# The second half of the sample's mLSTM states: from TensorE in the mixers to VectorE in the MLP

## The chip, the cores and the metric

The kernel runs on one core of a Trainium2 chip. The metric is the device time of one execution in microseconds (us); lower is better. The engines are called by their names in the profile: PE is TensorE (matmuls; PEld its weight loads), DVE is VectorE, ACT is ScalarE, POOL is GpSimd, SP is SyncE, which issues nearly all DMAs here.

## The reference, cut to what matters

One layer of a hybrid decoder runs on 256 prompt tokens and on 8 samples of 8 new tokens each, 320 columns in all. Two mixers (mLSTM with 4 heads, HGRN2 with 8) read one input projection; their gated outputs are merged and projected, and an MLP with a layer norm before and after follows:

```python
proj = jnp.einsum('btd,de->bte', x, w_in)
...
h, C, n, m = _mlstm(q, k, v, ig, lf, C0.astype(f32), n0.astype(f32), m0.astype(f32))
...
x1 = _layernorm(DEEPNORM_ALPHA * x + mix, ln1_g, ln1_b)
hid = jnp.square(jax.nn.relu(jnp.einsum('btd,df->btf', x1, w_up)))
ff = jnp.einsum('btf,fd->btd', hid, w_down)
y = _layernorm(DEEPNORM_ALPHA * x1 + ff, ln2_g, ln2_b)
return y, C.astype(dt), n.astype(dt), m.astype(dt), S.astype(dt)
```

The change is about the state C of the mLSTM. Each sample and each head has one of 256 x 512 (key x value). It is read for the outputs, and its new value is an output of the layer:

```python
num = jnp.einsum('bhts,bhsv->bhtv', s, vc) + w_inter[..., None] * jnp.einsum('bhtk,bhkv->bhtv', qc, C)
...
C_new = decay[..., None, None] * C + jnp.einsum('bhs,bhsk,bhsv->bhkv', w_end, kc, vc)
```

For a sample the sum over s has 8 terms, its 8 new tokens. Nothing else in this execution uses C_new.

## The kernel before, in words

All large products are made of tiles: 128 output channels by 320 columns, contracted over 2048 in 16 steps k. fp32 accuracy comes from splitting each operand into a high and a low part, so a step is three matmuls (high x high, low x high, high x low), called main matmuls below. There are 304 tiles (`TILES`): the mixers' projections and gates first, then the branch and output projections, then the MLP in four rounds of 16 up tiles and 16 down tiles. A tile's weights come in two units of 128 x 1024. A unit is loaded into one of three raw buffers (`wr`), ScalarE makes its high part and VectorE subtracts for its low part (`prep` and `low_half`). The pairs of high and low go into three buffers (`wh`, `wl`); from the output projection on, five more pairs (`wx`, tile `bb`) are used as well. `give` hands a pair back after its last matmul.

Everything else is written as Python generators (chains) and put between the main matmuls by `Sched`, a planner that runs when the program is built. It keeps an expected time for each engine, takes the chains in order of priority, and lets an instruction through when the engine and the operands are expected to be free. What it makes is a fixed order for each engine; the chip then goes by semaphores.

For each mLSTM head, the sample's part goes as follows. `m_states` loads the head's states in 16 chunks of 128 x 512 (8 samples times the first or second 128 rows, c = 0 or 1) into a pool of 14 buffers `cb`; from the second head on, two loads are 2.6 us apart. `m_KW` and `fourfold` bring the weighted keys of the samples to tokens in rows, four times over, in `kst`. `m_sample` then issues two lumps, each for four samples: some small sums (`m_few`), eight products of queries with the chunks (the matmuls `bank<-f` and `bank<-rx,f` of 512 columns), and `m_sums`, four matmuls of 32 rows that give the outer products of keys and values for c = 0 in four banks. `m_update` lets VectorE put each into its chunk (decay times chunk plus sum), then issues `m_sums` again for c = 1 into the same banks, and updates those chunks. `m_store` writes each chunk out.

At the end of the program `m_C` makes the prompt's final C from all 256 keys and values, which it loads through GpSimd's queue: heads 0 and 1 into freed weight buffers of `bb` and `wh`, `wl`, heads 2 and 3 into `wr` after the last weights are split.

Of the kernel before, what the change touches and what calls it, by code (L numbers as in the profile page):

```python
# [151 lines left out]
class Sched:  # L152
    PE_SIDE = 900.0

# [17 lines left out]
    def step(self, c, now):  # L172
        if c.req is None:
            try:
                c.req = c.gen.send(c.send)
            except StopIteration:
                c.done = True
                return False
            c.send = None
        kind = c.req[0]  # L180
        if kind == "wait":
            for e in c.req[1]:
                if e.t is None:
                    return False
            c.ready = max([c.ready] + [e.t for e in c.req[1]])
            c.eng = None
        elif kind == "acq":
            pool, n = c.req[1], c.req[2]
            if len(pool.free) < n:
                return False  # L190
            pool.free.sort(key=lambda x: x[0])
            got, pool.free = pool.free[:n], pool.free[n:]
            c.ready = max([c.ready] + [x[0] for x in got])
            c.eng = None
            c.send = got[0][1] if n == 1 else [x[1] for x in got]
        elif kind == "rel":
            c.req[1].free.append((c.ready, c.req[2]))
        elif kind == "set":
            c.req[1].t = c.ready
        else:  # L200
            _, cost, fn, *after = c.req
            r = max(after[0]) if after else c.ready
            if c.eng != kind or after:
                r += LAT
            elif kind in ("act", "dve"):
                r += SAME
            if kind == "pe":
# [9 lines left out]
            end = self.use(kind, r, cost)  # L217
            fn()
            c.ready, c.eng, c.send = end, kind, end
        c.req = None  # L220
        return True
# [20 lines left out]
def wait(*evs):  # L242
    return ("wait", evs)
# [60 lines left out]
class Program:  # L304
# [49 lines left out]
    def carve(self):  # L354
# [39 lines left out]
        self.kst = Pool([R.three(2, 256)])  # L394
# [82 lines left out]
    def carve_b(self):  # L477

        self.bb = self.pool.tile([128, 10240], F32R, name="bb", tag="f1")
        R = self.Part(self.bb)  # L480
        self.bbh, self.bbl = R.three(KT, TOK), R.three(KT, TOK)
        R = self.Part(self.bb)
        wide = [R(2048) for _ in range(5)]
        self.wx = [(w[:, 0:1024], w[:, 1024:2048]) for w in wide]
        self.wxv = wide
# [115 lines left out]
    def give(self, u):  # L601

        now, hl = self.s.t["pe"], self.unit[u][0]
        if FIRST <= u < 2 * FIRST:
            return
        wide = any(hl is w for w in self.wx)
        rest = self.next_prep >= len(UNITS)
        if u + 16 < len(UNITS) or not (rest or (self.n_vx < 3 if wide else self.n_kx < 1)):
            self.hl_free.append((now, hl))
        elif wide:  # L610
            self.n_vx += 1
            self.vx.free.append((now, self.wxv[[hl is w for w in self.wx].index(True)]))
        else:
            self.n_kx += 1
            self.kx.free += [(now, x.rearrange("p (x s k) -> p x s k", x=2, s=2)) for x in hl]
# [16 lines left out]
    def before(self, i, t):  # L632
# [16 lines left out]
        elif kind == "hg" and h == 0:  # L649
# [3 lines left out]
            f2 = self.pool.tile([128, 2320], F32, name="f2l", tag="f2a")  # L653
# [7 lines left out]
        elif kind == "wo" and h == 0:  # L661
# [4 lines left out]
            s.spawn(self.ln_x(), 1)  # L666
        elif kind == "dn" and c == 3 and h == 0:
# [420 lines left out]
    def m_KW(self, h):  # L1088
# [31 lines left out]
        yield from self.fourfold(self.kD[h][256:320], kst)  # L1120
        t = yield acq(self.khl)
        yield from self.high_low(kst.rearrange("p g k -> p (g k)"), t, 0)
# [71 lines left out]
    def m_C(self, h):  # L1194

        late = h >= 2
        if late:

            yield wait(self.rest_ev)
            x = self.wr.rearrange("p u n -> p (u n)")[:, 1536 * (h - 2):1536 * (h - 1)]  # L1200
            xk, xv = x[:, 0:512].rearrange("p (s k) -> p s k", s=2), x[:, 512:1536]
        else:
            k = yield acq(self.kx)
            w = yield acq(self.vx)
            xk, xv = k[:, 1].bitcast(F32), w[:, 1024:2048].bitcast(F32)
        tk = yield ("pool", 1000, lambda: self.nc.gpsimd.dma_start(xk, self.kD[h][0:256].rearrange("(s p) k -> p s k", p=128)))
# [3 lines left out]
        ek, e = Ev(), Ev()  # L1210
        ek.t, e.t = (tk, t + 500.0) if late else (t + 5000.0, t + 5000.0)
        yield wait(ek)
# [3 lines left out]
        if late:  # L1216
            w = yield acq(self.vx)
        yield wait(e)
        yield from self.split(xv, w[:, 0:1024], w[:, 1024:2048], 1024)
# [183 lines left out]
    def m_states(self, h):  # L1403
# [3 lines left out]
        for n in range(2 * NB):  # L1407
            b, c = self.state(n)
            cb = yield acq(self.cb)
            t = yield ("sp", 620, lambda: self.dma(cb, self.d["C0"][h, b, :, 512 * c:512 * c + 512]))  # L1410
# [12 lines left out]
    def m_sums(self, h, n, ps):  # L1423
# [3 lines left out]
        b, c = self.state(n)  # L1427
        g = b // 4
        for x in range(4):
            self.mm(ps[x], kst[32 * x:32 * x + 32, g, 128 * c:128 * c + 128], vst[32 * x:32 * x + 32, g, :], start=True, stop=True)  # L1430

    def m_update(self, h, n, cbs, ps):

        v, m = self.nc.vector, self.mh[h]
        for i in (n, n + 4):
            b, c = self.state(i)
            if i > n:
                yield ("pe", PE_4 + pe_r(512), lambda: self.m_sums(h, i, ps))
            for x in range(4):
                cb, p, bx = cbs[i - n + x], ps[x], b + x  # L1440
                t = yield ("dve", dve(512, True, 1, 1), lambda: v.scalar_tensor_tensor(cb, cb, m["bc"][:, 704 + bx:705 + bx], p, ALU.mult, ALU.add))
                self.s.spawn(self.m_store(h, i + x, cb), 3, t)
        for p in ps:
            yield rel(self.sbank, p)

    def m_store(self, h, n, cb):
        m = self.mh[h]
        b, c = self.state(n)
        yield ("sp", 620, lambda: self.dma(self.d["Cs"][h, b, :, 512 * c:512 * c + 512], cb))
        yield post(m["inter"][n])  # L1450
        yield wait(self.later(2500))
        yield rel(self.cb, cb)

# [842 lines left out]
    def run(self, pool):  # L2296
# [7 lines left out]
        self.wx, self.n_vx, self.n_kx = [], 0, 0  # L2304
# [4 lines left out]
        self.skD = [self.dr.tile([256, 128], F32, name=f"skD{j}") for j in range(HH)]  # L2309
        self.kD = [self.dr.tile([TOK, 256], F32, name=f"kD{j}") for j in range(MH)]  # L2310
# [14 lines left out]
    C0=(MH, NB, 128, 1024), S0=(HH, 128, NB, HV), cst=(128, C_END), lmask=(128, N_MASK),  # L2325
# [3 lines left out]
    Cs=(MH, NB, 128, 1024), Ss=(HH, 128, NB, HV),  # L2329
# [9 lines left out]
def lay_out(x_prompt, x_sample, state_mlstm_C, state_mlstm_n, state_mlstm_m, state_hgrn_S, hg_lb_logits, w_in,  # L2339
# [7 lines left out]
    for n, (i, half) in enumerate(UNITS):  # L2347
# [15 lines left out]
        C0=f(state_mlstm_C)[0].reshape(NB, MH, 2, 128, DV).transpose(1, 0, 3, 2, 4).reshape(MH, NB, 128, 1024),  # L2363
# [3 lines left out]
def take_out(r):  # L2367
# [9 lines left out]
        c(r["Cs"].reshape(MH, NB, 128, 2, DV).transpose(1, 0, 3, 2, 4).reshape(1, NB, MH, DK, DV)),  # L2377
# [21 lines left out]
```

## Time and profile before

| | before |
|---|---|
| median of 3 runs | 2251.0 us (2249.63 to 2251.93) |
| span of the profiled execution | 2246.3 us |
| PE busy | 2240.6 us |
| DVE busy | 1445.7 us |
| ACT busy | 1012.3 us |
| moved by DMA | 432.56 MB, mean 193 GB/s |

The span reaches from the first to the last instruction of one profiled execution; the runs' times hold what lies around it too, and the page gives no other time of that execution. The mixers last until about 810 us, the branch and output projections until about 1320 us, the MLP until 2222 us, and a tail with the final states and the last layer norm until the end. A busy time is the time in which at least one instruction of the engine or group was at work; matmuls overlap, so the distance between two starts tells more of their cost than their duration.

### The profile page before, as it was taken

Reading aid. Unit: us, or ns where it says so; the run is one execution under the profiler, and the core shown is the slowest. Engines: PE = TensorE matmul, PEld = TensorE weight load, DVE = VectorE, ACT = ScalarE, POOL = GpSimd, SP = SyncE. Lnnn points to the kernel's source line nnn. Section 1 sums busy time; section 2 is a strip of 40 time slices with the busy share of each in tenths; the row PEclk is TensorE's granted clock in tenths of the full one; section 3 lists DMA queues with packets and bytes.
Section 4 is the critical chain, followed back from the end, with each engine's and each line's share of the span. In section 5 each row is a group of like instructions: output and inputs, shape, how many; then the busy total and the mean of one; then the engine's idle time right before and its main releaser. Section 6 shows DMA issues by size and latency. Waiting matters only on the chain.

```text
span 2246.3 us, 40624 instructions
## 1 busy us (share of the span) xinstructions
PE 2240.6 (100%) x16218; PEld 2210.0 (98%) x16218; DVE 1445.7 (64%) x2584; ACT 1012.3 (45%) x1527; POOL 21.0 (1%) x53
## 2 busy tenths in 40 slices
PE   9999999999999999999999999999999999999999
PEld 9999999999999999999999999999999999999998
DVE  6768667888888887666556778444444444444566
ACT  5444444554555555444334456333432343234434
POOL 0000000000000000000000000000000000000001
PEclk9999999999999999999999999999999999999999
DMA  7998897776677754444446544444444444444554
GB/s 252 298 279 276 246 289 246 221 238 213 212 232 229 223 188 175 173 173 174 174 174 220 183 144 158 152 148 150 152 150 148 149 151 150 149 149 151 186 170 160
DMA packets 284982, 432.56 MB, mean 193 GB/s; under 512 B 136420, under 2 KB 181744, under 8 KB 284792
## 3 DMA queue, kind: packets, MB, share of 16 engines
q1 hardware_dynamic: 283832, 426.82, 57.3%
q0 software_dynamic: 960, 3.15, 0.5%
q8 instruction: 127, 2.08, 0.3%
q14 instruction: 63, 0.52, 0.1%
HBM read 380.52 MB, written 49.34 MB: 191 GB/s over the span
## 4 chain that ended last, share of the span: by engine, by line
PE 98%; DMA 1%; ACT 0%; SPq 0%; issue 0%; DVE 0%; POOL 0%; ACTq 0%; DVEq 0%; POOLq 0%
PE bank L348 98%; DMA wr<-wt 1%; DMA ra<-kD 0%; SPq L351 0%; ACT wh L342 0%; ACT f L342 0%; DVE wl L520 0%; DVE f L2066 0%; DVE f3m L2241 0%; DVE f2l L2065 0%; ACT misc L342 0%; DVE oS L1832 0%; ACT oS L342 0%; DVE f L966 0%; DVE f L1487 0%
## 5 line engine op out<-in xcount | busy, mean ns | idle before, releaser
L348 PE MATMUL bank<-xh,wh 128*128 128x320 f32 x2408 | 743.7, 310 | 0.0
L348 PE MATMUL bank<-xh,wl 128*128 128x320 f32 x2408 | 743.4, 310 | 0.0
L348 PE MATMUL bank<-xl,wh 128*128 128x320 f32 x2408 | 740.1, 308 | 0.0
L342 ACT ACTIVATE wh<-wr 128x1024 fp32r<-128x1024 f32 x424 | 448.5, 1058 | 588.3 <-PE bank L348 554.9
L520 DVE TENSOR_TENSOR wl<-wr,wh 128x1024 fp32r<-128x1024 f32 x423 | 516.8, 1222 | 293.2 <-ACT wh L342 288.6
L348 PEld LDWEIGHTS bank<-xh,wh 128*128 128x128 f32 x2408 | 452.6, 188 | 5.0 <-issue 3.9
L348 PEld LDWEIGHTS bank<-xl,wh 128*128 128x128 f32 x2408 | 452.1, 188 | 1.9
L348 PEld LDWEIGHTS bank<-xh,wl 128*128 128x128 f32 x2408 | 453.2, 188 | 0.0
L342 ACT ACTIVATE bb<-wr 128x1024 fp32r<-128x1024 f32 x181 | 191.8, 1061 | 353.9 <-PE bank L348 337.7
L520 DVE TENSOR_TENSOR bb<-wr,bb 128x1024 fp32r<-128x1024 f32 x179 | 219.0, 1224 | 157.4 <-ACT bb L342 157.3
L348 PE MATMUL bank<-rxb,bb 128*128 128x320 f32 x1264 | 287.7, 308 | 0.0
L348 PE MATMUL bank<-xh,bb 128*128 128x320 f32 (+1 forms) x1280 | 284.1, 309 | 0.0
L348 PE MATMUL bank<-ra,bb 128*128 128x320 f32 x1112 | 270.5, 308 | 0.0
L348 PE MATMUL bank<-ra,wh 128*128 128x320 f32 x968 | 259.4, 308 | 0.0
L348 PEld LDWEIGHTS bank<-xh,bb 128*128 128x128 f32 x1280 | 214.6, 188 | 0.0
L348 PEld LDWEIGHTS bank<-rxb,bb 128*128 128x128 f32 x1264 | 213.6, 188 | 0.0
L348 PE MATMUL bank<-xl,bb 128*128 128x320 f32 (+1 forms) x640 | 197.5, 309 | 0.0
L348 PEld LDWEIGHTS bank<-ra,bb 128*128 128x128 f32 x1112 | 190.7, 188 | 0.0
L348 PEld LDWEIGHTS bank<-ra,wh 128*128 128x128 f32 x968 | 172.5, 188 | 0.0
L348 PE MATMUL bank<-rxb,wl 128*128 128x320 f32 x520 | 160.3, 308 | 0.0
L348 PE MATMUL bank<-rxb,wh 128*128 128x320 f32 x520 | 160.3, 308 | 0.0
L348 PEld LDWEIGHTS bank<-xl,bb 128*128 128x128 f32 x640 | 120.2, 188 | 0.0
(343 smaller groups left out, 2132.7 us busy)
## 6 DMA issues: line engine op xcount, KB each, us to landing
wr<-wt SPq DMA_DIRECT2D x602, 512.0 KB, 3.2
rx<-C SPq DMA_DIRECT2D x34, 256.0 KB, 5.2
Cs<-rx SPq DMA_DIRECT2D x34, 256.0 KB, 5.4
f<-C SPq DMA_DIRECT2D x30, 256.0 KB, 5.1
Cs<-f SPq DMA_DIRECT2D x30, 256.0 KB, 4.5
f<-S SPq DMA_DIRECT2D x8, 512.0 KB
f3h<-S SPq DMA_DIRECT2D x8, 512.0 KB
Ss<-f SPq DMA_DIRECT2D x8, 512.0 KB, 4.8
```

The costliest lines, as they stand in the source:

```text
L342: return self.nc.scalar.activation(out, in_, func, **kw)
L348: self.nc.tensor.matmul(*a, **kw)
L520: self.V().tensor_tensor(lo, raw, hi.bitcast(F32), ALU.subtract)
```

## The change

The chunks with c = 1 are still loaded in the mixers for the product with the queries, but are neither updated nor stored there. `m_update` gives them free at once, and updates c = 0 only; `kst` holds the first 128 columns of the keys.

The c = 1 half is updated during the MLP. From the up tile 12 of the first round on, the five `wx` pairs are no longer given back to the weights (`retire`); the three pairs `wh`, `wl` go on alone. When all five are back, their memory becomes the tile `fu`, and a chain `m_late` for each head runs, one head after the other. It copies the sample's values to a DRAM tensor `vsD`, and loads them back with the eight tokens of a sample in each of its 16 partitions, in four DMAs that wait between each other. It loads the keys and the decays in the same form (8 samples x 16 partitions, 8 rows of the state in each). Then four parts of two rows each, of 512 KB, are loaded; ScalarE multiplies a part by the decay, and VectorE adds 8 tokens x 2 rows with one instruction each, of 128 x 512. The part is stored in one DMA. These VectorE instructions have a class of their own, `bg`: the planner lets one through only if VectorE is expected to be free within 250 ns. For four heads that makes 256 of them, with 16 on ScalarE, 16 loads and 16 stores of 512 KB, 16 loads of values of 512 KB, and 40 small DMAs.

The end values of all four heads are loaded into their final places: the values into four buffers in `f1` that are free after the last `m_late`, the keys of heads 0 and 1 there too, those of heads 2 and 3 into a part of `f2l`. The layout of C0 and Cs in DRAM becomes head, half, sample, row, value.

```diff
@@ Sched.step
+            if kind == "bg":
+                if (r > now and c.eng != kind) or self.t["dve"] > now + self.BG:
+                    return False
@@ give
-        wide = any(hl is w for w in self.wx)
-        rest = self.next_prep >= len(UNITS)
-        if u + 16 < len(UNITS) or not (rest or (self.n_vx < 3 if wide else self.n_kx < 1)):
+        if self.spare is not None and any(hl is w for w in self.wx):
+            self.retire(now, hl)
+        elif self.next_prep < len(UNITS):
             self.hl_free.append((now, hl))
...
@@ m_KW
-        yield from self.fourfold(self.kD[h][256:320], kst)
+        yield from self.fourfold(self.kD[h][256:320, 0:128], kst)
@@ m_update
-        for i in (n, n + 4):
-            b, c = self.state(i)
-            if i > n:
-                yield ("pe", PE_4 + pe_r(512), lambda: self.m_sums(h, i, ps))
-            for x in range(4):
-                cb, p, bx = cbs[i - n + x], ps[x], b + x
-                t = yield ("dve", dve(512, True, 1, 1), lambda: v.scalar_tensor_tensor(cb, cb, m["bc"][:, 704 + bx:705 + bx], p, ALU.mult, ALU.add))
-                self.s.spawn(self.m_store(h, i + x, cb), 3, t)
-        for p in ps:
+        b = self.state(n)[0]
+        for x in range(4):
+            yield post(m["inter"][n + 4 + x])
+            yield rel(self.cb, cbs[4 + x])
+        for x in range(4):
+            cb, p, bx = cbs[x], ps[x], b + x
+            t = yield ("dve", dve(512, True, 1, 1), lambda: v.scalar_tensor_tensor(cb, cb, m["bc"][:, 704 + bx:705 + bx], p, ALU.mult, ALU.add))
+            self.s.spawn(self.m_store(h, n + x, cb), 3, t)
             yield rel(self.sbank, p)
@@ m_late_part (new; called by m_late for q = 0 to 3, 4 us apart)
+        of, to = (self.d[n][h, 1].rearrange("b (d r) v -> (b d) r v", r=8)[:, 2 * q:2 * q + 2] for n in ("C0", "Cs"))
+        c = yield acq(self.lc)
+        cb = c.rearrange("p (r v) -> p r v", r=2)
+        yield ("sp", 620, lambda: self.dma(cb, of))
+        yield wait(self.later(9000), e)
+        yield ("act", act(1024, False, 1), lambda: self.A(c, c, scale=k[:, 64:65]))
+        for t in range(NT):
+            for r in range(2):
+                x, y = v[t // 4][:, t % 4, :], k[:, 8 * t + 2 * q + r:8 * t + 2 * q + r + 1]
+                yield ("bg", dve(512, False, 1, 1), lambda: self.nc.vector.scalar_tensor_tensor(cb[:, r], x, y, cb[:, r], ALU.mult, ALU.add))
+        yield ("sp", 620, lambda: self.dma(to, cb))
...
```

How the instructions stand, at three places. The first is TensorE in the last mLSTM head, behind its second lump. `bank<-xh,wh` and the like are main matmuls, `bank<-ra` of 512 columns to four banks in a row are `m_sums`. Before, the four for c = 1 stand by themselves between main matmuls:

```order
L348 MATMUL bank_84<-xh,wl 128x320
L348 MATMUL bank_90<-ra 128x512
L348 MATMUL bank_89<-ra 128x512
L348 MATMUL bank_85<-ra 128x512
L348 MATMUL bank_86<-ra 128x512
L348 MATMUL bank_84<-xh,wh 128x320
```

After, only the four that end a lump, right behind its state products:

```order
L352 MATMUL bank_88<-f_79 32x512 x2
L352 MATMUL bank_89<-ra 128x512
L352 MATMUL bank_87<-ra 128x512
L352 MATMUL bank_86<-ra 128x512
L352 MATMUL bank_90<-ra 128x512
L352 MATMUL bank_83<-xh,wh 128x320
```

In all, the matmuls of 512 columns out of `ra` go from 108 to 76, and TensorE's other counts stay. Between the two lumps of a head stood 87 main matmuls; now there are 36 in the first head and 57 in the others.

The second place is VectorE in the first round of down tiles (`wl<-wr,wh` and `bb<-wr,bb` are the weights' subtractions, one for a unit; `f3m<-f3m,bank` takes a finished tile out of its bank). Before:

```order
L2241 TENSOR_TENSOR f3m<-f3m,bank_88 128x320
L520 TENSOR_TENSOR bb<-wr,bb 128x1024
L520 TENSOR_TENSOR wl<-wr,wh 128x1024
L2241 TENSOR_TENSOR f3m<-f3m,bank_85 128x320
L520 TENSOR_TENSOR wl<-wr,wh 128x1024 x2
```

After:

```order
L523 TENSOR_TENSOR wl<-wr,wh 128x1024
L1513 SCALAR_TENSOR_TENSOR fu<-fu 128x512 x3
L523 TENSOR_TENSOR wl<-wr,wh 128x1024
L1513 SCALAR_TENSOR_TENSOR fu<-fu 128x512
L2306 TENSOR_TENSOR f3m<-f3m,bank_85 128x320
L1513 SCALAR_TENSOR_TENSOR fu<-fu 128x512 x2
```

Three or four updates `fu<-fu` now stand between two subtractions, and all subtractions write `wl`, since `bb` is retired. They come in four stretches of some 20 units, one for each head, with 12 units or so between them.

The third place is SP behind the first lump of the first head, where `f_79<-C` are the loads of the chunks that use buffers given free by that lump. Before:

```order
L351 DMA wr<-wt 128x1024 x2
L351 DMA gaD_164<-f_78 128x320
L351 DMA Cs<-f_79 128x512 x3
L351 DMA wr<-wt 128x1024
L351 DMA f_79<-C 128x512
```

After:

```order
L355 DMA wr<-wt 128x1024 x2
L355 DMA f_79<-C 128x512 x2
L355 DMA Cs<-f_79 128x512 x2
L355 DMA gaD_168<-f_78 128x320
L355 DMA Cs<-f_79 128x512 x2
```

The loads stood behind three stores of updated chunks, whose buffers they reuse; now they stand ahead of the stores, behind the weight loads.

More of the change, by code (lines that the diff above doesn't have):

```diff
@@ L652, in before @@
             self.carve_b()
-            f2 = self.pool.tile([128, 2320], F32, name="f2l", tag="f2a")
+            f2 = self.f2l = self.pool.tile([128, 2320], F32, name="f2l", tag="f2a")
             B = self.Part(f2)
@@ L1452, in m_store, with retire @@
         yield rel(self.cb, cb)
+    def retire(self, now, hl):
+        self.spare.append(hl)
+        if len(self.spare) == len(self.wx):
+            A = self.Part(self.pool.tile([128, 10240], F32, name="fu", tag="f1"))
+            self.lv, self.lc, self.lk = (Pool([]) for _ in range(3))
+            self.lv.free = [(now, A.three(4, 512)) for _ in range(2)]
+            self.lc.free = [(now, A(1024)) for _ in range(5)]
+            self.lk.free = [(now, A(80)) for _ in range(2)]
+            for h in range(MH):
+                self.s.spawn(self.m_late(h), 8)
```

102 lines of the change are left out of this document (69 added, 33 removed).

## The prediction

> **What bounds the kernel now.** I read the page first, then the waits of TensorE, then the stages, then single places in time.
>
> ```profile
> span 2246.3 us, 40624 instructions
> PE 2240.6 (100%) x16218; PEld 2210.0 (98%) x16218; DVE 1445.7 (64%) x2584; ACT 1012.3 (45%) x1527; POOL 21.0 (1%) x53
> PE 98%; DMA 1%; ACT 0%; SPq 0%; issue 0%; DVE 0%; POOL 0%; ACTq 0%; DVEq 0%; POOLq 0%
> ```
>
> TensorE (PE) is busy for all but 5.7 us, and 98% of the chain that ends last is its own matmuls. Its waits for other engines are these and no more:
>
> ```profile
> PE bank L348 <- POOL ones L689: 1.0, 1, 1.0
> PE bank L348 <- DVE f2l L2065: 0.4, 1, 0.4
> PE bank L348 <- ACT oS L342: 0.4, 1, 0.4
> PE bank L348 <- ACT misc L342: 0.2, 1, 0.2
> ```
>
> So an edit shortens the run only by taking work off TensorE, and lengthens it only by making TensorE wait. The stages (columns: stretch, then busy us of PE, PEld, DVE, ACT, POOL, then clock, DMA share and GB/s) show how much room stands beside it:
>
> ```profile
> 100.00:400.00 300.00, 300.00 (x2148) 282.53 (x2147) 216.31 (x408) 136.42 (x218) 0.00 (x0) 1.00 0.87 271
> 400.00:800.00 400.00, 400.00 (x3427) 392.92 (x3426) 348.08 (x896) 214.41 (x400) 5.04 (x17) 1.00 0.73 220
> 1400.00:1600.00 200.00, 200.00 (x1367) 200.00 (x1366) 89.92 (x101) 72.25 (x87) 0.00 (x0) 1.00 0.42 151
> 1600.00:1800.00 200.00, 200.00 (x1367) 200.00 (x1366) 88.35 (x97) 70.14 (x81) 0.00 (x0) 1.00 0.42 150
> 1800.00:2000.00 200.00, 200.00 (x1367) 200.00 (x1367) 89.25 (x99) 71.32 (x83) 0.00 (x0) 1.00 0.42 150
> 2000.00:2222.00 222.00, 222.00 (x1518) 222.00 (x1517) 122.85 (x166) 89.60 (x118) 8.98 (x12) 1.00 0.46 157
> ```
>
> The last four rows are the MLP: 200.00 us over 1367 matmuls gives 0.146 us for one, VectorE (DVE) works 45% of the time (55% at the end) and DMA moves 150 GB/s. The first two rows are the mixers. There VectorE is busy up to 87% and DMA reaches 271 GB/s, with the same three weight buffers that the MLP is to be left with, and TensorE is busy throughout all the same.
>
> **The change part by part.** Eight groups of four 32-row matmuls go from TensorE (two for each of four heads, those of the second 128 rows of the states). One of them in time, with the main matmuls around it:
>
> ```profile
> 280.10 0.31 PE L348 MATMUL bank<-xh,wl 128*128 128x320 f32 x1
> 280.34 0.51 PE L348 MATMUL bank<-ra 32*128 32x512 f32 x4
> 280.77 0.41 PE L348 MATMUL bank<-xh,wh 128*128 128x320 f32 x1
> 281.03 0.31 PE L348 MATMUL bank<-xl,wh 128*128 128x320 f32 x1
> L348 PE MATMUL bank<-ra 32*128 32x512 f32 x64 | 8.6, 495 | 0.2 <-ACT misc L342 0.2
> ```
>
> From 280.10 to the second main matmul behind the group is 0.93 us; two steps of 0.146 us would have done without it. It costs 0.64 us, and eight cost 5.1 us. The last row, whose 64 matmuls are busy for 8.6 us, gives the other end: half of them is 4.3 us, without the slow entry and exit. I take 5.1, since the starts of the neighbours contain everything that the group holds up. [...]
>
> The groups that stay, one at the end of each lump (a lump is the run of small sample matmuls of one head), are as before. In the first head one of them waits for ScalarE (ACT), which copies the small results out of its bank:
>
> ```profile
> 90.70 0.51 PE L348 MATMUL bank<-ra 32*128 32x512 f32 x3
> 91.44 0.50 PE L348 MATMUL bank<-ra 32*128 32x512 f32 x1 [0.23 <-ACT misc L342]
> ```
>
> That is 0.74 us. The lump comes nine main matmuls (1.3 us) earlier now, and the two copies stand two ScalarE instructions further forward. I take no change, between 0.7 us won and 0.7 us lost. The halved doubling of k (128 instead of 256 columns) and the 32 updates and stores that leave the mixers are on VectorE, ScalarE and the SP queue, where TensorE waits for nothing: zero, and nothing back if that cover were thinner, since this is less work.
>
> The lumps move closer together: 36 main matmuls between the two of the first head and 57 in the later heads, where 87 stood. The second lump reads state chunks whose buffers the first one gives free, so a load must fit between.
>
> ```profile
> DMA to landing us min/median/max: 3.6/5.2/7.1
> L351 SPq DMA_DIRECT2D rx<-C x34: 328/431/1525, 70.8 to 377.3; - x34
> 271.62 0.31 PE L348 MATMUL bank<-misc,f 128*32 128x1 f32 x16
> 272.34 1.46 PE L348 MATMUL bank<-rx,f 128*32 128x512 f32 x10
> 273.73 0.50 PE L348 MATMUL bank<-ra 32*128 32x512 f32 x4
> ```
>
> The first two rows are all loads of these states, from issue to landing and in the SP queue; the others are one lump. Its state matmuls end just before 273.73, and the last chunk is read some 1.3 us behind the lump's start (an estimate from these rows). In the first head there are thus 36 x 0.146 + 1.3 = 6.6 us, for two issues of 0.43 us and a landing of 5.2 us: 6.1 us, which fits by 0.5. At 7.1 us TensorE would wait 1.4 us. In the later heads there are 9.6 us for 2.6 us of spacing (a constant in the code), one issue and the landing, 8.2 us; at 7.1 us it would be a wait of 0.5 us each. The bounds are 0 and 2.9 us, and I take 0, as the median landing fits everywhere.
>
> In the MLP VectorE gets 256 updates, ScalarE 16 scalings and SP about 90 issues. What they lie beside is this (the first down projection; 385 to 388 us is the mixers, for the price of an update):
>
> ```profile
> 1502.28 1.23 DVE L520 TENSOR_TENSOR wl<-wr,wh 128x1024 fp32r<-128x1024 f32 x1 [2.30 <-ACT wh L342]
> 1504.86 0.49 DVE L2241 TENSOR_TENSOR f3m<-f3m,bank 128x320 f32<-128x320 f32 x1 [1.35 <-PE bank L348]
> 1505.81 1.23 DVE L520 TENSOR_TENSOR bb<-wr,bb 128x1024 fp32r<-128x1024 f32 x1 [0.46 <-ACT bb L342]
> 386.59 0.74 DVE L1441 SCALAR_TENSOR_TENSOR f<-f,f2a,bank 128x512 f32<-128x512 f32 x1
> 387.25 0.48 DVE L1488 SCALAR_TENSOR_TENSOR f<-f 128x320 f32<-128x320 f32 x1
> L1441 DVE SCALAR_TENSOR_TENSOR rx<-rx,f2a,bank x34: 729/742/749, 102.8 to 395.4; 128x512 f32<-128x512 f32 x34
> L342 ACT ACTIVATE wh<-wr 128x1024 fp32r<-128x1024 f32 x424 | 448.5, 1058 | 588.3 <-PE bank L348 554.9
> wr<-wt SPq DMA_DIRECT2D x602, 512.0 KB, 3.2
> ```
>
> The nearest row to the new update is L1441, the same operation on 512 columns: 0.742 us alone, but the next instruction starts 0.66 us behind it. 256 x 0.66 = 169 us, against 432 us that VectorE has free from 1400 to 2222 us (822 less the busy times of the four rows above). What counts is the packing: each weight unit (24 main matmuls, 3.5 us) now has three or four updates beside it. A tile of the down projection then asks 2 x 1.15 (a weight subtraction, 1.23 less the same overlap) + 0.41 + 6.25 x 0.66 = 6.8 us of VectorE in 7.0, and one of the up projection 2 x 1.15 + 0.82 + 6 x 0.66 = 7.1 us in 7.0. VectorE is full for the 20 or so units that each head takes. With three weight buffers left, a buffer given back has two units, 7.0 us, until its next weights are wanted; ScalarE takes 1.06, VectorE may be busy with one update and a little more (0.9), the subtraction takes 1.23. That leaves 3.8 us for lateness, so I take 0. The DMA adds 8 MB of states read again, 8 MB of v and 8 MB of stores over some 110 units: 65 GB/s on 150, still below the 271 that the second mixer stage carried; a weight load of 3.2 us has three units to land in. The 16 scalings of ScalarE (about 17 us) fall into its idle half. Zero for all, and 0 to 7.6 us as the bounds (the first rival).
>
> The end values' loads start eight tiles before the end and their splits come earlier; TensorE's order of matmuls in the tail is the same as before, except for buffer names. Zero, within 0.5 us either way.
>
> The sum against the profiled execution: 2246.3 - 5.1 = 2241.2 us of span. The median of the runs stands 4.7 us above that span, and the change leaves what lies outside it alone: 2251.0 - 5.1 = 2245.9, rounded to **2246.0 us**. About 0.2% of this time (4.5 us) is what a measurement can tell from no change, so the forecast lies just outside it.
>
> **The rivals.** First, slower or as before: VectorE, packed in the MLP, falls behind and TensorE waits for weights. If the updates did not overlap their neighbours, each would cost 0.742 us instead of 0.66, 64 of them 5.2 us more for a head; above the 3.8 us of slack that is 1.4 us of waiting, 5.6 us for four heads, and the time 2251.5. At 0.749 us it is 2253.5. It turns the gain into a loss from 0.739 us on, and passes 0.2% from about 0.76 us. For it speaks the full VectorE; against it that L1441 overlaps, and that 87% busy cost TensorE nothing from 400 to 800 us. Second, the state loads are late at the second lumps: up to 2.9 us back, 2247 to 2249. For it speaks the short distance in the first head, against it the median landing. Third, more is won: the wait of 0.74 us in the first head goes, 2245 or a little under. That the change does not do what it says is ruled out by the order of instructions, where 32 of the 108 matmuls of 512 columns out of that tile are gone.
>
> **How the numbers follow.** The forecast has a chance of 0.55 (2245 to 2247.3), the late state loads 0.17, a VectorE that eats the gain or a little more 0.12, a loss beyond 0.2% 0.08 (the same rival with late loads on top, 2256 to 2262), more gain 0.08. Some of the forecast's own spread, 0.13, ends above 2246.5. So faster by over 0.2% is 0.42 + 0.08 = 0.50, slower 0.08, and the rest 0.42. The range goes from 2244.0 (the third rival and half a microsecond) to 2252.0 (the first rival's first price), which leaves out less than 2 in 10.
>
> **What would show it.** The profile after should have 32 of the 32-row matmuls of 512 columns, a mean distance of main matmuls in the MLP still at 0.146 us, no TensorE wait for a weight buffer, VectorE near 95% in four stretches of 70 us between 1455 and 1875 us (counted back from the end of the main matmuls by tiles of 7.0 us), and the second lumps of about 2.4 us. I am wrong if a lump stands longer than that (late state loads), or if the MLP windows hold fewer than 1367 matmuls in 200 us (weights late).

## The result, and the profile after

The change makes the kernel slower: 2290.28 us median of 4 runs (2284.83 to 2290.71), against 2251.47 us (2249.63 to 2252.57) for the kernel before, measured with it. The ratio is 1.0169, 95% interval [1.0154, 1.0183]. The forecast was 2246.0 us with a range up to 2252.0.

The page of the kernel after has these lines in place of the three that the prediction opened with:

```profile
span 2288.0 us, 40787 instructions
PE 2251.5 (98%) x16186; PEld 2220.3 (97%) x16186; DVE 1582.2 (69%) x2808; ACT 1029.4 (45%) x1543; POOL 21.1 (1%) x53
PE 92%; DMA 6%; DVE 1%; ACT 1%; issue 0%; SPq 0%; POOL 0%; ACTq 0%; DVEq 0%; POOLq 0%
```

TensorE is now idle for 36.5 us instead of 5.7, and 6% of the chain that ends last is DMA. The list of waits (total us, times, longest) says what TensorE waits for, and what that engine waits for in turn:

```profile
PE bank L352 <- ACT wh L346: 26.3, 6, 6.5
PE bank L352 <- DVE wl L523: 3.9, 8, 0.9
ACT wh L346 <- DMA wr<-wt: 117.6, 32, 11.2
```

TensorE waits for ScalarE's high parts of weights, and ScalarE for the weight loads. VectorE, on which the first rival had put the loss, hardly appears. The stages of the kernel after (the MLP now ends at 2263 us):

```profile
100.00:400.00 300.00, 300.00 (x2138) 287.54 (x2137) 201.26 (x391) 141.18 (x225) 0.00 (x0) 1.00 0.82 242
1400.00:1600.00 200.00, 186.02 (x1225) 183.91 (x1225) 112.95 (x147) 62.81 (x71) 0.00 (x0) 0.95 0.62 174
1600.00:1800.00 200.00, 193.40 (x1298) 192.74 (x1298) 162.73 (x220) 73.98 (x84) 0.00 (x0) 0.97 0.61 187
1800.00:2000.00 200.00, 192.73 (x1295) 191.81 (x1295) 124.76 (x162) 74.48 (x90) 1.60 (x2) 0.97 0.58 177
```

The mixers are as busy as they were. In the MLP 1225 to 1298 matmuls stand in 200 us instead of 1367, and the granted clock of TensorE is below 1.00: something stops TensorE, and its clock drops.

The main matmuls, 14,600 in both kernels, serve as a common scale, as worked out from the starts in the two traces; the 9,101st stands in the MLP ahead of the late loads, the 14,001st behind the last of them. The 9,101st starts at 1416.54 us before and at 1411.36 us after: the mixers won 5.2 us. From it to the 14,001st TensorE takes 718.0 us before and 762.3 us after: 44.2 us lost. From there to the 14,596th, in the tail, it is 87.3 us before and 89.3 us after, 2.1 us lost. The sum, 41.1 us, is the difference of the spans (41.7) but for 0.6 us. Below, "MLP" and "tail" with a number mean these two distances.

One stop in the kernel after, the first late head's, on TensorE:

```profile
1468.25 0.31 PE L352 MATMUL bank<-rxb,wl 128*128 128x320 f32 x1
1474.16 0.64 PE L352 MATMUL bank<-rxb,wh 128*128 128x320 f32 x1 [5.61 <-ACT wh L346]
1476.12 0.47 PE L352 MATMUL bank<-ra,wh 128*128 128x320 f32 x1
1476.39 0.47 PE L352 MATMUL bank<-rxb,wl 128*128 128x320 f32 x1
```

TensorE stands for 5.9 us, and then starts a matmul every 0.27 us instead of 0.147. There is one such stop in each of the four heads (5.8, 6.6, 6.4 and 6.5 us beyond the usual distance), each followed by work at clock 0.50. SP's queue ahead of that stop (`wr<-wt` are the weight loads, `fu<-vsD` the loads of the values, called v below, `fu<-C` those of the states):

```profile
1438.89 0.59 SPq L355 DMA_DIRECT2D fu<-vsD  x1
1442.04 0.33 SPq L355 DMA_DIRECT2D wr<-wt  x1
1442.42 0.59 SPq L355 DMA_DIRECT2D fu<-vsD  x1
1445.56 3.85 SPq L355 DMA_DIRECT2D wr<-wt  x2
1449.46 0.59 SPq L355 DMA_DIRECT2D fu<-vsD  x1
1450.11 2.10 SPq L355 DMA_DIRECT2D fu<-C  x4
1458.02 31.66 SPq L355 DMA_DIRECT2D wr<-wt  x8
```

The four loads of the states stand in one row. The code's pause between the parts (`yield wait(self.later(4000))`) does not space them: it counts from SP's last use, which does not move while the loop spawns the four parts, so all four become ready together. And this is what the DMA engines do there, with the stops of the four heads below (columns as in the stages; the last two are the share of the DMA engines and GB/s):

```profile
1440.00:1445.00 5.00, 5.00 (x36) 5.00 (x35) 2.41 (x3) 1.82 (x2) 0.00 (x0) 1.00 0.92 215
1450.00:1465.00 15.00, 14.68 (x100) 14.41 (x99) 4.56 (x5) 3.18 (x3) 0.00 (x0) 1.00 1.03 222
1469.00:1474.00 5.00, 0.00 (x0) 0.00 (x0) 0.00 (x0) 0.95 (x1) 0.00 (x0) 0.68 0.52 212
1590.00:1595.00 5.00, 0.16 (x1) 0.16 (x1) 0.18 (x1) 1.27 (x2) 0.00 (x0) 0.53 0.51 209
1719.00:1724.00 5.00, 0.12 (x1) 0.12 (x1) 0.14 (x1) 1.23 (x2) 0.00 (x0) 0.60 0.51 209
1842.00:1846.00 4.00, 0.00 (x0) 0.00 (x0) 0.00 (x0) 0.00 (x0) 0.00 (x0) 0.61 0.51 209
```

First the DMA engines are full for 15 us. Then, while TensorE stands, their share is one half in all four heads (0.51 or 0.52), as if half of the engines were working off a queue and the other half had nothing to do. The landings shown with the last experiments, eight parts of a load early and eight late, bear this out.

### The profile page after: what moved, and what is told of

Same layout as the page of the kernel before. It is cut to its first block, busy times and chain, and to the rows that moved or that the text cites. A ratio compares the mean times of both kernels' runs of the same rounds, so it can differ in the third digit from the quotient of the medians.

```text
span 2288.0 us, 40787 instructions
## 1 busy us (share of the span) xinstructions
PE 2251.5 (98%) x16186; PEld 2220.3 (97%) x16186; DVE 1582.2 (69%) x2808; ACT 1029.4 (45%) x1543; POOL 21.1 (1%) x53
## 4 chain that ended last, share of the span: by engine, by line
PE 92%; DMA 6%; DVE 1%; ACT 1%; issue 0%; SPq 0%; POOL 0%; ACTq 0%; DVEq 0%; POOLq 0%
PE bank L352 92%; DMA wr<-wt 5%; DMA fu<-vsD 1%; DVE wl L523 1%; ACT wh L346 1%; DMA f<-sD 0%; DVE xhs L1983 0%; DVE f3m L2306 0%; DVE xls L1983 0%; SPq L355 0%; ACT xls L346 0%; ACT xhs L346 0%; DVE f L2131 0%; DVE rh L2085 0%; DVE f2l L2130 0%
## 5 line engine op out<-in xcount | busy, mean ns | idle before, releaser
L523 DVE TENSOR_TENSOR wl<-wr,wh 128x1024 fp32r<-128x1024 f32 x563 | 687.7, 1222 | 399.5 <-ACT wh L346 396.4
L352 PE MATMUL bank<-xh,wh 128*128 128x320 f32 (+1 forms) x2896 | 896.0, 310 | 13.0 <-ACT wh L346 13.0
L352 PE MATMUL bank<-xh,wl 128*128 128x320 f32 (+1 forms) x2896 | 897.1, 311 | 2.0 <-DVE wl L523 2.0
L352 PE MATMUL bank<-xl,wh 128*128 128x320 f32 (+1 forms) x2896 | 893.0, 309 | 0.0
L352 PE MATMUL bank<-ra,wh 128*128 128x320 f32 x1728 | 475.0, 311 | 6.2 <-ACT wh L346 6.2
L352 PE MATMUL bank<-rxb,wh 128*128 128x320 f32 x1024 | 318.8, 311 | 7.0 <-ACT wh L346 7.0
L352 PE MATMUL bank<-rxb,wl 128*128 128x320 f32 x1024 | 318.7, 311 | 1.6 <-DVE wl L523 1.6
L352 PEld LDWEIGHTS bank<-rxb,wh 128*128 128x128 f32 x1024 | 194.5, 190 | 7.6 <-ACT wh L346 7.6
L352 PEld LDWEIGHTS bank<-rxb,wl 128*128 128x128 f32 x1024 | 194.3, 190 | 2.5 <-DVE wl L523 2.5
L1513 DVE SCALAR_TENSOR_TENSOR fu<-fu 128x512 f32<-128x512 f32 x256 | 179.8, 746 | 0.3 <-ACT fu L346 0.3
```

The costliest lines, as they stand in the source:

```text
L352: self.nc.tensor.matmul(*a, **kw)
L523: self.V().tensor_tensor(lo, raw, hi.bitcast(F32), ALU.subtract)
L1513: yield ("bg", dve(512, False, 1, 1), lambda: self.nc.vector.scalar_tensor_tensor(cb[:, r], x, y, cb[:, r], ALU.mult, ALU.add))
```

## The experiments

Theory: weight loads that stand behind the rows of late loads come too late for three pairs of buffers. Rivals: the packed VectorE, three pairs as such, the added bytes wherever they are put. What makes a row of loads so slow was found only by the second and third rounds. The kernel before ran beside each round, with medians of 2251.34, 2251.01 and 2250.85 us.

### The four state loads 8 us apart

```diff
@@ m_late
+        at = self.s.t["sp"]
         for q, x in enumerate(evs):
-            yield wait(self.later(4000))
-            self.s.spawn(self.m_late_part(h, q, v, k, e, x), 9)
+            self.s.spawn(self.m_late_part(h, q, v, k, e, x), 9, at + 8000.0 * (q + 1))
```

> The changed kernel with one difference: a head's four state loads of the MLP (fu<-C, 512 KB each) are issued 8 us apart instead of in one row. Theory (burst): in the changed kernel TensorE stands for about 6 us in each of four heads, because a weight load sits in the DMA queues behind four value loads and four state loads, and its clock is then granted at half for 10.24 us; together some 41 us, and some 5 us more in the tail. With the loads apart the four stops go: about 2250 us, of which 5 us is the tail. Rival (VectorE packing): the 256 updates are as dense as before, so TensorE still waits for weights, 2285 us or so. Rival (value loads alone): the four value loads are unchanged; if they do it, half or more of the stops stay, 2265 to 2285 us.

Measured: 2249.55 us (2248.4 to 2254.89, 8 runs), ratio 0.9994 [0.9983, 1.0004]. The stops of 6 us are gone, and so is the low clock in the MLP. The waits in this kernel:

```profile
PE bank L352 <- ACT wh L346: 1.7, 2, 1.1
ACT wh L346 <- DMA wr<-wt: 98.9, 42, 6.5
ACT xhs L346 <- DMA f<-sD: 6.9, 1, 6.9
```

The same work and bytes, placed otherwise, give back 41 us. In this profile 6.5 us are left in the MLP (724.6 us) and 1.8 in the tail (89.1): two places with `fu<-vsD` ahead of them, and one around 2136 to 2147 us, where loads for the end values run together.

### Three weight pairs alone

The kernel before, with only this part of the change: the five `wx` pairs are retired at the up tile 12 of the first round, and the c = 1 half stays in the mixers.

```diff
@@ give (in the kernel before; retire as in the changed one, into the places of the end values)
+        if wide and self.spare is not None:
+            return self.retire(now, hl)
...
```

> The kernel before with one difference: from the up tile 12 of the first round on the five extra weight pairs are not given back to the weights (they go to the end values when these come), so that the MLP runs on three pairs, with no late state update. Theory (burst): three pairs suffice when nothing else is in the DMA queues: 2251 us within 0.2%, perhaps up to 5 us more from the tail, where loads for the HGRN states come in a row. Rival (three pairs are too few): TensorE waits for weights all through the MLP, 2260 us or more.

Measured: 2253.7 us (2252.93 to 2256.52), ratio 1.0012 [1.0001, 1.0022]. MLP 718.0 us, tail 87.3: exactly as before. Three pairs cost TensorE nothing while only weights are loaded. The 2.4 us between the medians are not in these two stretches; in the profile the extra time stands in the mixers, where the edit changes nothing (the 9,101st main matmul starts at 1421.04 us).

### The loads without the work

The changed kernel without the 16 scalings and the 256 updates. The loads and stores stay, so the second half of the new states is not computed.

```diff
@@ m_late_part
-        yield ("act", act(1024, False, 1), lambda: self.A(c, c, scale=k[:, 64:65]))
-        for t in range(NT):
-            for r in range(2):
-                ...
+        yield wait(self.later(20000 + 10000 * q))
```

> The changed kernel without the scalings on ScalarE and the 256 updates on VectorE: values, keys and states are loaded at the same places in the SP queue, and the states are stored unchanged (the second half of the sample's new states is left out). Theory (burst): the stops of TensorE are as before, four of about 6 us with the clock at half behind them, 2285 to 2290 us. Rival (VectorE packing): the stops go with the updates, about 2246 to 2251 us.

Measured: 2282.86 us in one run, 2 us below what was expected, MLP 756.2 us. So 38.2 of the 44.2 us lost in the MLP stand without a single update on VectorE. The stops are there, again with half of the DMA engines in the second head's and the last head's:

```profile
PE bank L352 <- ACT wh L346: 20.9, 6, 6.3
1559.00:1564.00 5.00, 0.00 (x0) 0.00 (x0) 0.00 (x0) 0.06 (x1) 0.00 (x0) 0.88 0.53 215
1744.00:1748.00 4.00, 0.35 (x3) 0.09 (x1) 0.00 (x0) 0.73 (x1) 0.00 (x0) 0.89 0.52 211
```

### The mixers' half alone

The kernel before, with the `m_sums`, updates and stores for c = 1 taken out of the mixers and nothing put into the MLP: the second half of the new states is left out.

```diff
@@ m_update (as in the change)
-                yield ("pe", PE_4 + pe_r(512), lambda: self.m_sums(h, i, ps))
@@ m_KW
-        yield from self.fourfold(self.kD[h][256:320], kst)
+        yield from self.fourfold(self.kD[h][256:320, 0:128], kst)
...
```

> The kernel before with the mixers' half of the change alone: the states' second 128 rows are neither updated nor stored (this part of the new states is left out), the keys are brought over for 128 columns only, and the eight groups of four 32-row matmuls are gone. Weight buffers, MLP and end values are as before. The prediction's main term: 5.1 us less, 2246 us, ratio 0.9977. Rival (only the busy share of these matmuls counts): 4.3 us less. Rival (the second lumps come too early for their state loads): up to 2.9 us of it lost, 2248 to 2249 us.

Measured: 2245.04 us (2244.02 to 2248.97), ratio 0.9974 [0.9964, 0.9985], 6.3 us between the medians. The list of TensorE's waits stays short:

```profile
PE bank L348 <- ACT misc L342: 0.8, 1, 0.8
L348 PE MATMUL bank<-ra 32*128 32x512 f32 x32 | 5.1, 495 | 0.8 <-ACT misc L342 0.8
```

The gain that was forecast is there within the interval (3.4 to 8.1 us by the ratio), and no lump waits for a state.

### The tail's loads spread

The spaced kernel above, with the keys and values of the four heads begun 32, 28, 11 and 5 tiles before the end instead of all at 8. (The expectation says units; the code counts tiles.)

```diff
@@ before
+        for j, n in enumerate((32, 28, 11, 5)):
+            if i == len(TILES) - n:
+                s.spawn(self.m_C(j), 3)
-        elif i == len(TILES) - 8:
-            for j in range(MH):
-                s.spawn(self.m_C(j), 3)
```

> a_spaced with the tail alone mended: the end values' GpSimd loads of the four heads begin 32, 28, 11 and 5 units before the end instead of all at 8; the v loads stay 3.5 us apart. Theory: the tail gaps of a_spaced (0.8, 1.05 and 1.68 us) go, the 8.3 us of the MLP stay: 2246 to 2248 us. If the tail's gaps come from the state sums that are loaded there in before as well, no change: 2249 to 2250 us, and ScalarE still waits some 7 us for one of those loads.

Measured: 2246.0 us (2244.04 to 2248.5), ratio 0.9977 [0.9967, 0.9987]. MLP 718.0, tail 87.3 us. ScalarE's wait for `f<-sD` falls from 6.9 to 1.8 us. The MLP's leftover went too, though its loads are placed as in the spaced kernel: the profiled executions, of 2254.89 us there and 2244.04 us here, are the two ends of what was measured, so with v every 3.5 us single executions seem to lie on both sides of the edge. How much of the 3.5 us between the medians is the tail's stays open.

### Every late load by itself

The same, and the loads of v 8 us apart.

```diff
@@ m_late
-            yield wait(self.later(3500))
+            yield wait(self.later(8000))
```

> The changed kernel with every late load by itself: the four 512 KB loads of C of a head 8 us apart, the four loads of v of a head 8 us apart instead of 3.5, and the four heads' key and value loads for the end values begun 32, 28, 11 and 5 units before the end instead of all at 8. Theory (a load of weights that stands behind a row of other loads comes too late): the 37 us of stops are gone as in a_spaced, the pieces left there (8.3 us by the TensorE pitch from 1400 to 2150, 3.5 us of tail gaps) go too, and what is left is the mixers' gain: 2245 to 2247 us, ratio to before 0.9972 to 0.998, no TensorE gap over 0.3 us between 1400 and 2150, no interval of clock 0.5 there. Rival (VectorE's 256 updates, or the total of DMA traffic, cost TensorE time however the loads are placed): it stays near a_spaced, 2249 to 2251 us, with ScalarE's and VectorE's lateness spread over the four heads.

Measured: 2244.85 us (2243.99 to 2249.35), ratio 0.9969 [0.9957, 0.9981]. MLP 718.0, tail 87.3 us. With all of the work done this version beats the kernel before, as the one ahead of it does; the second pause did not move the median by more than the runs differ. The profiled execution took 2249.35 us, with its extra time in the mixers, so it is read for the MLP alone:

```profile
1400.00:1600.00 200.00, 200.00 (x1367) 200.00 (x1366) 124.77 (x162) 71.64 (x86) 0.00 (x0) 1.00 0.57 176
1495.00:1540.00 45.00, 45.00 (x309) 45.00 (x308) 44.78 (x61) 16.61 (x16) 0.00 (x0) 1.00 0.56 198
1447.20:1448.40 1.20, 1.20 (x10) 1.20 (x9) 0.52 (x1) 0.00 (x0) 0.00 (x0) 1.00 0.53 140
```

The second row is a head's updates: VectorE busy for 44.78 of 45 us, and TensorE starts 309 matmuls, its full pace. The third lies within one load of v and almost wholly between the packets of two weight loads: share 0.53. That led to the last two kernels below.

### Rows of copies, with three and with eight pairs

Do rows of any loads stop TensorE? In the MLP, rows of 1, 2, 3, 4, 5, 6, 8 and 10 copies from DRAM to DRAM of 512 KB each, 20 weight units apart, in the kernel with three pairs and in the kernel before.

```diff
+    def burst(self, n):
+        for k in range(n):
+            x = self.dr.tile([128, 1024], F32, name=f"bD{n}_{k}")
+            yield ("sp", 620, lambda: self.dma(x, self.d["C0"][k % MH, k // MH]))
@@ before
+        n = {196: 1, 206: 2, 216: 3, 226: 4, 236: 5, 246: 6, 256: 8, 266: 10}.get(i)
+        if n:
+            s.spawn(self.burst(n), 3)
```

> The kernel before with five of its eight weight pairs retired at the MLP (as in b_three), and in the MLP eight rows of extra 512 KB copies from DRAM to DRAM on SP's queue, 20 weight units apart: 1, 2, 3, 4, 5, 6, 8 and 10 of them in a row (one weight load between the fourth and the fifth). Nothing waits for the copies. Theory: a weight load that stands behind n copies comes n x 3.2 us late (the time of a 512 KB load alone) if a copy costs the DMA engines as much as a load, and 3.8 to 7 us of it are covered by three pairs: no stop at 1, a stop of 0 to 3 us at 2, 3 to 6 us at 3, about 6 to 9 at 4, growing by some 3.2 us for each further copy, to about 25 us at 10; each stop over 3 us is followed by a time at clock 0.5. If a copy costs twice a load (it reads and writes), the first stop comes at 1 or 2 and each further copy adds 6.4 us. Rival (a row of loads is shared out among the queues and hides): no stop at any n up to 4.

> The same rows of copies in the kernel before with all its eight weight pairs. Theory: five pairs more cover 5 x 3.5 = 17.5 us more, so 21 to 25 us in all: no stop up to 6 copies, none or a small one at 8, at most some 8 us at 10 (at twice the price of a copy: the first stop at 4 or 5). Rival (the pairs do not matter, the queue does): the same stops as with three.

Measured, one run each: 2254.96 us with three pairs, 2253.83 with eight; MLP 718.9 us with three, 718.0 with eight. Most of what the two executions take beyond the kernel before lies in the mixers. With three pairs the theory missed and its rival held: no stop up to eight copies in a row, and 0.9 us at ten. The granted clock stays at 1.00 there (1980 to 1985 us); no stop was over 3 us, so what the expectation says of the clock behind such stops was not tried by this run. With eight pairs nothing is lost in the MLP, within what was expected there. SP's queue, ScalarE's splits (the high parts of the weights, with the waits ahead of them) and the DMA share around the ten copies, with three pairs:

```profile
1958.55 2.65 SPq L351 DMA_DIRECT2D bD<-C  x4
1961.69 0.70 SPq L351 DMA_DIRECT2D wr<-wt  x1
1962.43 3.97 SPq L351 DMA_DIRECT2D bD<-C  x4
1967.31 0.33 SPq L351 DMA_DIRECT2D wr<-wt  x1
1968.37 1.72 SPq L351 DMA_DIRECT2D bD<-C  x2
1966.38 1.06 ACT L342 ACTIVATE wh<-wr 128x1024 fp32r<-128x1024 f32 x1 [2.46 <-PE bank L348]
1971.58 1.06 ACT L342 ACTIVATE wh<-wr 128x1024 fp32r<-128x1024 f32 x1 [4.14 <-DMA wr<-wt]
1978.69 1.06 ACT L342 ACTIVATE wh<-wr 128x1024 fp32r<-128x1024 f32 x1 [6.05 <-DMA wr<-wt]
1982.63 1.06 ACT L342 ACTIVATE wh<-wr 128x1024 fp32r<-128x1024 f32 x1 [2.88 <-DMA wr<-wt]
1960.00:1980.00 20.00, 20.00 (x139) 20.00 (x138) 6.00 (x7) 4.65 (x5) 0.00 (x0) 1.00 0.96 357
```

Splits usually start 3.52 us apart, so the fourth one would start at 1976.94: it is 5.7 us late, and TensorE loses 0.9. So three pairs cover some 5 us. The ten copies and the weight loads among them take 20 us at 357 GB/s. A row of transfers is thus not enough; the theory in that general form is refuted, and what is different about the late loads must be found. Where the kernel after ran at full share, it moved only 222 GB/s, and then the share fell to one half.

### v from 16 rows, and v further apart

The loads of v read, for each of 8 samples, one row of 4 KB into 16 partitions: the outer dimension is 8. In the first kernel v is stored twice in DRAM, so that a load reads 16 rows into 8 partitions each (the second copy is made by eight small transfers in place of one); everything else is the changed kernel, rows and all. In the second only the pause between the loads of v is 8 us, and the four state loads still follow in a row.

```diff
@@ m_late (first kernel; vsD has twice the rows)
-        yield ("sp", 620, lambda: self.dma(self.vsD[h].rearrange("t (j k) -> t j k", j=4), ...))
+        w = self.vsD[h].rearrange("(b c t) (j k) -> c b t j k", c=2, t=NT, j=4)
+        for c2 in range(2):
+            for j in range(4):
+                yield ("sp", 620, lambda: self.dma(w[c2][:, :, j], ...))
...
-            yield ("sp", 620, lambda: self.dma(v[i // 2][...], at(x)))
+            yield ("sp", 620, lambda: self.dma(v[i // 2][...], x.unsqueeze(1).to_broadcast([16, 8, 1024])))
@@ m_late (second kernel)
-            yield wait(self.later(3500))
+            yield wait(self.later(8000))
```

> The changed kernel with its loads in the same places (v 3.5 us apart, the four of C in a row), but the v of a head is stored twice in DRAM, by eight small transfers instead of one, so that a load of v reads 16 different rows instead of 8. In the changed kernel the share of the DMA engines stands at 0.50 to 0.52 for five to seven microseconds of each stop. Theory A (a load with 8 outer rows is carried by 8 of the 16 engines; the halves of weight loads queue up behind v on these): that stretch at one half goes, the backlog drains on 16 engines instead of 8, so the stops of some 6 us shrink to 3 us or less and the times at clock 0.5 with them: 10 to 24 us of excess in place of 41, 2255 to 2274 us. Theory B (only the bytes and the order of the row count): the same stops as before, 2283 to 2291 us.

> The changed kernel with the loads of v 8 us apart instead of 3.5, the last of them still followed by the four loads of C in a row. Theory A (v's eight engines hold a backlog that builds up over the four loads of v): most of the stop goes, since the backlog drains between them; left is the last v and the row of C, 2.5 MB, some 7 to 10 us of the DMA engines of which 4 to 5 are covered: stops of 0 to 4 us a head, 2248 to 2268 us. Theory B (the row of C alone makes the stop): the stops of 5.8 to 6.6 us stay in all four heads, 2280 to 2290 us.

Measured: with 16 rows 2249.17 us (2247.72 to 2250.17), ratio 0.9985 [0.9974, 0.9996]; with the pause 2253.57 us (2250.23 to 2256.19), ratio 1.0006 [0.9992, 1.002]. With 16 rows no stop is left in the four heads: the MLP's 719.9 us hold 1.8 us too much, all of it behind 2129 us, and the tail takes 91.1. That is better than theory A's 10 to 24 us, and far from theory B. SP's queue and the DMA share, first head:

```profile
1453.87 0.53 SPq L355 DMA_DIRECT2D fu<-vsD  x1
1454.45 2.05 SPq L355 DMA_DIRECT2D fu<-C  x4
1457.02 15.54 SPq L355 DMA_DIRECT2D wr<-wt  x5
1450.00:1465.00 15.00, 15.00 (x104) 15.00 (x103) 5.87 (x6) 4.25 (x4) 0.00 (x0) 1.00 1.00 301
1465.00:1469.00 4.00, 4.00 (x30) 4.00 (x29) 0.49 (x1) 0.40 (x1) 0.00 (x0) 1.00 1.02 404
```

The four state loads are still in one row, but the bytes go at 301 and 404 GB/s instead of 222, the queue is empty by 1471 us, and the stretch at one half is gone. The packed trace also records when the parts of a transfer land. A weight load lands in 16 parts; a load of v lands in eight with 8 rows (besides one record a microsecond after its issue) and in 16 with 16 rows. In the kernel after, the weight load that the first stop waits for is issued at 1458.02 us; eight of its parts have landed by 1466.19, the other eight only from 1472.59 to 1472.95, and ScalarE splits it at 1473.05. In the four heads the eighth and the last part lie 6.8, 7.7, 5.8 and 6.2 us apart, and the stops are 5.8, 6.6, 6.4 and 6.5 us. With 16 rows the first weight load behind the states, issued at 1457.02, lands from 1466.93 to 1468.50.

So it is the loads of v, which land in eight parts, that make the row too long: eight landings and then a share of 0.51 to 0.52 with 8 rows, 16 landings and a share of 1.02 up to 1469 us with 16. That the outer dimension sets how many engines carry a load is the author's reading of these two cases; no other dimension was tried. With the pause, which by theory A was to let the queue on v's eight engines drain between loads, 6.9 us in the MLP and 4.4 in the tail are left, within the range that theory A gave. A rival that blamed the row of states alone is refuted by both. Nor are the loads of v enough by themselves: with the states spaced, and v as it was, the stops of 6 us went too.

## Why the prediction was right or wrong

**The matmuls that leave TensorE: right.** 5.1 us were forecast; the 9,101st main matmul came 5.2 us earlier, and the mixers' half alone won 6.3 us of medians. That 5.2 comes so close is partly luck: in the seven profiled kernels that have these mixers, the 9,101st starts between 1411.36 and 1417.06 us. The 32-row matmuls are down to 32 as said, and the waits that were left open did not come. The first head's lumps after (the last group of the first one, then the second lump's first small sums and its group):

```profile
89.76 0.51 PE L352 MATMUL bank<-ra 32*128 32x512 f32 x4
96.38 0.24 PE L352 MATMUL bank<-misc,f 128*32 128x1 f32 x8
98.30 0.51 PE L352 MATMUL bank<-ra 32*128 32x512 f32 x4
```

The second lump takes 1.92 us to its group and 2.4 in all, as said: its states were there. The first lump's group now stands in one piece, so the break of 0.74 us between two starts (0.23 us of it idle) went in this execution; where the mixers' half is done alone, TensorE is idle for 0.8 us there.

**VectorE in the MLP: right.** The 256 updates took 179.8 us, 0.70 us each, where 0.66 and 169 us were said:

```profile
L1513 DVE SCALAR_TENSOR_TENSOR fu<-fu 128x512 f32<-128x512 f32 x256 | 179.8, 746 | 0.3 <-ACT fu L346 0.3
```

They fill VectorE in the stretches between the stops, and where the loads are placed otherwise that costs TensorE nothing. The first rival, and with it the 0.08 for a loss, rested on the wrong engine. No rival was about the DMA queue; only the last sign, fewer than 1367 matmuls in 200 us because weights are late, pointed at it, and it came true.

**The DMA in the MLP: wrong, and this is the step that failed.** It read: "65 GB/s on 150, still below the 271 that the second mixer stage carried; a weight load of 3.2 us has three units to land in." Three things in it do not hold. The 65 GB/s are an average over 110 units; per head, 2 MB of v and 2 MB of states were issued within some 17 us, and the fixed order of SP's instructions, which was there to be read, has the four state loads in one row. The 271 GB/s, of 100 to 400 us, were reached without such loads; a load of v lands in eight parts where a weight load lands in 16, the DMA share beside the stops is 0.51 or 0.52, and the first weight load behind the row, with eight parts landed by 1466.19 us, was split only when the other eight had landed too (1472.95). And "three units to land in" counted the buffers as if nothing stood ahead in the queue; measured, three pairs cover some 5 us, near the 3.8 us worked out from VectorE, while ScalarE stood up to 11.2 us for one load. The term was put at 0, with 7.6 us as its far end, and was 44.2 us in the profile: about 25 us of stops (5.8 + 6.6 + 6.4 + 6.5), and most of the rest work at half clock behind them, 25 us of it, which costs about half of its time (an estimate from the clock records and the first starts behind the stops).

**The tail: wrong by a little.** "TensorE's order of matmuls in the tail is the same" holds, and so the end was put at 0 ± 0.5 us. But the end values' loads, all begun in one place beside the state sums of the other mixer, hold ScalarE back, and weight splits stand behind it in its order:

```profile
2146.69 1.45 POOL L1211 DMA_DIRECT2D f2l<-kD  x2 [216.27 <-DVE f L2292]
2148.14 5.96 POOL L1213 DMA_DIRECT2D bbx<-vtD  x8
2168.62 2.31 ACT L346 ACTIVATE xhs<-f 128x768 fp32r<-128x768 f32 x3 [7.70 <-DMA f<-sD]
```

By the steps of the main matmuls this cost 4.9 us between 2150 and 2224 us (2.8 of them fall before the 14,001st and stand above as MLP's). Spreading those loads took away what the spaced kernel still had of it.

## What to carry to other kernels

Work that is moved beside a saturated engine brings its loads along, and what counted of those here was how long the DMA engines needed for the longest row ahead of the next urgent load, not the mean rate: read the printed order for rows, and compare their time with what the buffers cover. Ten copies in a row cost 0.9 us here, four loads of v and four of states 5.8 to 6.6 us a head and the low clock behind them. Count a transfer's outer dimension too: with 8 the loads of v landed in eight parts here and the DMA share stood at 0.51 or 0.52 during the stops, and of a weight load behind them the last part landed 5.8 to 7.7 us after the eighth; with 16 they landed in 16, the share behind the row was 1.02, and these stops were gone. A pause in a generator spaces loads only if the clock it counts from moves on.

## What the runs showed of the hardware

- A share of the DMA engines of 0.51 to 0.53 with a queue standing was the mark of loads that land in eight parts here. The 15 us ahead of the first stop show a share of 1.03 at only 222 GB/s, where the loads from 16 rows went at 301: a packet of 4 KB took 0.30 us on average there, 0.22 us with 16 rows, and 0.16 us during the stop. So the 16 rows changed two things, the number of parts that land (16 instead of eight) and the time of a packet. Why packets are slower beside v, and how much of the gain is due to each, stays open.
- Copies from DRAM to DRAM of 512 KB in packets of 32 KB went at 357 GB/s together with the weights, ten in a row for 0.9 us of TensorE.
- A stop costs more than its length. In the MLP the granted clock is 0.50 for 3.41, 6.83 or 10.24 us at a time: 10.24 after the stops of 5.8 to 6.6 us in the kernel after, 3.41 from 2173.98 us on in the same kernel, behind waits of 1.43 and 0.89 us, and 6.83 or 3.41 after the stops of 1.9 to 6.5 us with the loads alone. At 0.50 main matmuls start 0.267 us apart. In the first head the clock fell at 1470.84 us, 2.6 us after the last matmul had started, and came back at 1481.08, 6.9 us after the work did (1474.16), with a wait of 0.36 us in that time. What sets these times was not shown.
